# The gate unit's columns of the second half as seven block products in two passes

## The chip, the cores and the metric

One core of one Trainium2 chip runs the whole program. The metric is device time in microseconds (us): the median of the runs. Engines are TensorE (PE), VectorE (DVE), ScalarE (ACT), GpSimd (POOL) and SyncE (SP), which here issues nearly all DMAs.

## The reference, cut to what matters

One layer over 2048 latent tokens of width 1024 with a 256-token context ahead of it. One input projection `p = h @ w_in` with 3584 columns feeds two head groups:

```python
h = modulate(rmsnorm(x, norm_mix[l]), sh1, sc1)
p = h @ w_in[l]                       # 5 x 512 columns for the recurrence, 2 x 512 for the gate unit
...
def chunk_sgu(u, v, ln_g, ln_b, w_s, b_s):
    u = gelu(u); v = gelu(v)          # 4 heads of 128 channels, chunks of 128 positions
    v = layernorm(v, ln_g, ln_b)
    z = einsum('hpq,bnqhc->bnphc', w_s, v) + b
    return u * z
...
x = x + g1 * (o @ w_out[l])           # o: both groups side by side
x = x + g2 * conv_ffn(h2, ...)        # gated MLP with a 3x3 convolution
```

The other group (A) is a gated linear recurrence in both directions (four heads, 128 x 128 state). Only the gate unit's columns (B: u in columns 2560 to 3071, v in 3072 to 3583) change here, and of them only the second half of the tokens.

## The kernel before, in words

Everything is float32; a product that needs it is made of three `float32r` matmuls (`mm3`, L134): each operand is split (`split`, L129) into a high part (an ACT copy, L131) and a low part (a subtraction, L132), and high x high, high x low, low x high are summed in PSUM. A matmul takes 128 contraction rows, 128 columns of weights and 512 tokens.

The tokens are worked in two halves of 1024. For a half, `xh` and `xl` hold the normalised input's parts with the 1024 features on 8 blocks of 128 rows (NK = 8). **`x_second`** (L426) prepares half two while half one is being projected: in four groups of two token chunks it loads rows, scales them, transposes them on PE (64 transposes of 128 x 128), applies `a1`/`s1` (`x_mod`, L239), splits, and stores both parts in DRAM (`xh_d`, `xl_d`, L452). They are read back into `xh`/`xl` between the halves (L1074, L1075).

**The projection** runs as a list of banks (`run_banks`, L514). A bank is 512 tokens by 128 columns: 8 blocks x 3 matmuls = 24 matmuls into one of three `pj` PSUM banks, which a sink then evicts. Weights come raw from DRAM (`load_raw`, L211) and are split two keys ahead (`split_w`, L216). The banks' order is a string written by hand, for half two `f0 b0 f1 v0 b1 f2 u0 b2 f3 b3 v1 u1 v2 u2 v3 u3`: `f` is a recurrence head's front (gate `silu`, v, q: six banks, L977 to 978), `b` its back (forget gates: four banks), `v` and `u` the gate unit's two banks each.

**Two queues of generators** (`Pump`, L140s) are advanced at slots between the blocks of a bank, when PE's own counted time `T.t` has passed the wait that the generator yielded. `hg_q` holds the recurrence (`hg`, L776: scores by seven levels, states, output; `deferred`, L883: what half one's backward scan still lacks); each is posted at the start of the next front. `need` forces a queue ahead of its waits: `pre_q` needs the previous head's scores begun ("diag"), `pre_g` (ahead of the back) needs its keys, `pre_v` the end of the head before that. `bg_q` holds preparations: `x_start`, `misc`, `x_second`, then `ada_block` x8, `w_out_ops`, `conv_taps`, `w_down_ops`. A scheduler fixes each engine's order at build time by readiness in its model; `pin` keeps an instruction in program order.

**The gate unit** (`sgu`, L668): `su` evicts u by GELU, `sv` evicts v by GELU and queues `ln` after 4.6 us of `T.t` (transposes, statistics L694, L695, the root on POOL L126, normalisation L699) and then `mix` after 7.0 more (the position mixing on PE, L707); `both` multiplies on POOL (L675) and stores to `oT_d` (L676). Ahead of the second last pair of banks `open_wo` drains both queues, closes the pool of the recurrence's tiles and starts ten loads of the output projection's weights `wo` into that memory (L1106). Then comes the output projection, tile by tile (128 tokens), which fetches its operands with L1269.

PSUM has eight banks: three `pj`, two `sc`, three `mi`. Single or double buffers that matter: `raw` (three), `acc` (one), `sig` (two), `sgt` (two), `K` (two), `F` (one).

## Time and profile before

| | us |
|---|---|
| median of three runs (2453.74 to 2454.19) | 2453.82 |
| the profiled execution | 2449.13 |
| its span, first to last instruction | 2447.3 |
| half two's input stores (`xl_d`), first and last issue | 114.3, 201.9 |
| last matmul of the input projection | 977.3 |
| first load of the ten `wo` | 967.8 |

In a row of the grouped views stand line, engine, operation, tiles written and read, shapes and count, then busy time and mean ns of one, then the engine's idle time just before and who ended it. A row of windows has the length, then for PE, weight loads, DVE, ACT and POOL the busy time and count, then the granted clock, the DMA engines' busy share and GB/s. Matmuls are pipelined: their listed durations overlap, so their cost is read from how many fit in a stretch.

### The profile page before, as it was taken

What the parts mean: (1) busy time and instruction counts of PE and PEld (TensorE: products, weight loads), DVE (VectorE), ACT (ScalarE), POOL (GpSimd) and SP (SyncE); (2) the same over time, 40 slices, a digit from 0 to 9 for tenths busy, and PEclk for the clock granted to TensorE, in tenths of its full rate; (3) what the DMA queues carried; (4) which work ended last, traced back from release to release, by engine and by line L of the source; (5) the groups of instructions that cost most, each with busy time, mean ns of one, the idle gap of its engine ahead of it and who ended that gap; (6) DMA issues with size and microseconds to landing.
All of it is one profiled execution on the core that took longest, in us unless ns stands there. A gap on an engine that the chain in (4) does not pass through costs nothing.

```text
span 2447.3 us, 32836 instructions
## 1 busy us (share of the span) xinstructions
PE 2408.3 (98%) x11859; PEld 2000.8 (82%) x11859; DVE 1785.5 (73%) x2445; ACT 943.7 (39%) x1614; POOL 873.4 (36%) x795
## 2 busy tenths in 40 slices
PE   7999999999999999999999999999999999999998
PEld 4788888888888888788788888878888888888887
DVE  5867685756776776466698877769999992776875
ACT  4554334333344433354443333333333342332343
POOL 1232010110111122001688778787778870000002
PEclk9999999999999999999999999999999999999999
DMA  8365446564254234668822222562222238934645
GB/s 310 109 210 171 141 136 209 193 225 147 96 185 155 87 104 149 233 216 261 297 86 88 82 96 83 177 237 85 86 93 94 83 102 349 318 125 146 228 151 197
DMA packets 307855, 400.13 MB, mean 163 GB/s; under 512 B 33113, under 2 KB 216161, under 8 KB 304621
## 3 DMA queue, kind: packets, MB, share of 16 engines
q1 hardware_dynamic: 304404, 397.28, 48.1%
q8 instruction: 94, 1.54, 0.3%
q10 hardware_dynamic: 3289, 0.76, 0.1%
q14 instruction: 68, 0.56, 0.1%
HBM read 288.85 MB, written 109.13 MB: 163 GB/s over the span
## 4 chain that ended last, share of the span: by engine, by line
PE 40%; DVE 7%; issue 3%; POOL 2%; ACT 1%; DMA 0%; SPq 0%; POOLq 0%; ACTq 0%; DVEq 0%
PE up L65 25%; PE dn L65 15%; DVE dn L1377 3%; DVE edges L1382 1%; DVE gp L1458 1%; ACT dn L1374 1%; POOL Al L132 0%; POOL ra L1669 0%; POOL rr L1670 0%; DVE keep L1452 0%; POOL raw L1195 0%; DVE keep L1468 0%; ACT cv L1396 0%; ACT Ah L131 0%; POOL cv L1469 0%
## 5 line engine op out<-in xcount | busy, mean ns | idle before, releaser
L1377 DVE SCALAR_TENSOR_TENSOR dn<-gp,taps,dn 128x1024 f32<-128x1024 f32 x352 | 448.3, 1280 | 21.4 <-ACT dn L1374 18.1
L65 PE MATMUL up<-yf,Ah 128*128 128x512 f32 x1232 | 393.7, 389 | 0.0
L65 PE MATMUL dn<-thl,mhl 128*128 128x512 f32 x1680 | 381.5, 389 | 1.2 <-ACT thl L131 1.2
L132 POOL TENSOR_TENSOR Al<-raw,Ah 128x512 fp32r<-128x512 f32 x264 | 342.9, 1307 | 92.0 <-ACT Ah L131 79.0
L65 PEld LDWEIGHTS dn<-thl,mhl 128*128 128x128 f32 x1680 | 315.0, 188 | 67.7 <-ACT thl L131 2.0
L65 PE MATMUL pj<-xh,whi 128*128 128x512 f32 x896 | 363.1, 406 | 0.0
L65 PE MATMUL pj<-xh,wlo 128*128 128x512 f32 x896 | 350.6, 392 | 2.0 <-DVE wlo L132 2.0
L65 PE MATMUL pj<-xl,whi 128*128 128x512 f32 x896 | 351.4, 392 | 1.1 <-POOL xl L132 1.0
L65 PE MATMUL up<-xah,Al 128*128 128x512 f32 x704 | 275.6, 392 | 3.8 <-POOL Al L132 3.8
L65 PE MATMUL up<-xah,Ah 128*128 128x512 f32 x704 | 274.5, 390 | 0.6 <-ACT Ah L131 0.6
L65 PEld LDWEIGHTS up<-yf,Ah 128*128 128x128 f32 x1232 | 231.2, 188 | 48.1
L131 ACT CAST Ah<-raw 128x512 fp32r<-128x512 f32 x264 | 160.5, 618 | 278.4 <-PE up L65 208.4
L65 PE MATMUL up<-xal,Ah 128*128 128x512 f32 x528 | 205.5, 389 | 0.0
L65 PE MATMUL up<-yf,Al 128*128 128x512 f32 x528 | 205.2, 389 | 0.0
L65 PEld LDWEIGHTS pj<-xh,wlo 128*128 128x128 f32 x896 | 168.3, 188 | 38.2 <-DVE wlo L132 2.7
L65 PEld LDWEIGHTS pj<-xh,whi 128*128 128x128 f32 x896 | 168.6, 188 | 33.3 <-issue 3.5
L65 PEld LDWEIGHTS pj<-xl,whi 128*128 128x128 f32 x896 | 168.8, 188 | 32.2 <-POOL xl L132 1.9
L65 PE MATMUL dn<-wo,o 128*128 128x512 f32 x768 | 182.9, 394 | 2.1 <-ACT o L131 1.6
L580 POOL TENSOR_TENSOR K<-K,tot 128x512 f32<-128x512 f32 x40 | 50.0, 1251 | 343.9 <-PE sc L65 194.5
L65 PEld LDWEIGHTS dn<-wo,o 128*128 128x128 f32 x768 | 141.9, 188 | 31.8 <-ACT o L131 2.0
L65 PEld LDWEIGHTS up<-xah,Al 128*128 128x128 f32 x704 | 132.1, 188 | 36.5 <-POOL Al L132 9.4
L65 PEld LDWEIGHTS up<-xah,Ah 128*128 128x128 f32 x704 | 132.2, 188 | 28.0 <-ACT Ah L131 1.0
(315 smaller groups left out, 3923.7 us busy)
## 6 DMA issues: line engine op xcount, KB each, us to landing
raw<-in_w_up_dram SPq DMA_DIRECT2D x88, 512.0 KB, 4.7
mr<-m SPq DMA_DIRECT2D x85, 512.0 KB, 5.0
raw<-in_w_in_dram SPq DMA_DIRECT2D x68, 512.0 KB, 4.2
sT<-wd SPq DMA_DIRECT2D x88, 256.0 KB, 4.1
raw<-in_w_ada_dram SPq DMA_DIRECT2D x32, 512.0 KB, 3.8
yf<-yd SPq DMA_DIRECT2D x14, 1024.0 KB
m<-cv SPq DMA_DIRECT2D x22, 544.0 KB, 2.7
raw<-in_w_down_dram SPq DMA_DIRECT2D x22, 512.0 KB, 4.3
```

The lines of the kernel that those rows point to most:

```text
L65: return self.engine.matmul(out, lhsT, rhs, **kw)
L131: keep(S.copy(hi, raw))
L132: (eng or G).tensor_sub(lo, raw, hi.bitcast(F32))
L580: e.tensor_mul(view(K2, row * W + o, src), view(K, o, src), view(tot, t0, [[4, n], [ts, 2], [0, B]]))
L1374: S.activation(cr, gt[:, 0:RH, 0:GW], AF.Identity, bias=cvb[:, f:f + 1], scale=taps[:, f:f + 1])
L1377: V.scalar_tensor_tensor(out=cr, in0=gt[:, t // 3:t // 3 + RH, t % 3:t % 3 + GW], scalar=taps[:, t * NF + f:t * NF + f + 1], in1=cr, op0=A ...
L1382: V.scalar_tensor_tensor(out=e[:, 0, :], in0=gt[:, 1, t % 3:t % 3 + GW], scalar=taps[:, t * NF + f:t * NF + f + 1], in1=e[:, 0, :], op0=AL ...
L1458: V.tensor_add(g_rows(hh, f + c, n2), quad(p, kind), quad(add, kind))
```

## The change

For each gate head the two column groups (u, v) x the two halves of the 1024 features make a 2 x 2 block matrix of weights, and features x the two 512-token parts a 2 x 2 block matrix of inputs. Strassen's algorithm in Winograd's form takes seven block products of 12 matmuls in place of eight.

- `x_second` now takes chunks g and g + 4 together, forms the four sums and differences of input blocks next to the four blocks, splits all eight on DVE and stores them as eight operands (`xo_d`), 512-byte runs.
- `pair_ops`, new in `bg_q` ahead of the ada blocks, forms the seven weight operands per head, splits them and stores them (`sp_d`). `w_down_ops` yields 7.0 in place of 9.0.
- The recurrence's gate of half one goes straight to DRAM (`silu_out`); `x_second` and `pair_ops` use the `sgt` buffers in half one.
- Half two runs all recurrence heads first (the last with its gate columns at the end), then 28 products: pass one has products 0, 1, 2 of all heads, pass two 3, 4, 6, 5. Products load split weights three ahead and x quarters when the last user of the old ones is done. Partial sums (`u2_d`) and the finished u of the first part (`su_d`) wait in DRAM between the passes. `open_wo` comes ahead of the last seven products.

```diff
...
-    xh_d = dr.tile([P, NK, TH], F32, name="xh_d")
-    xl_d = dr.tile([P, NK, TH], F32, name="xl_d")
+    xo_d = dr.tile([P, 8, 2, 4, 512], F32, name="xo_d")
+    sp_d = [dr.tile([P, 7, 2, 512], F32, name=f"sp{h}") for h in range(NH)]
+    u2_d = [dr.tile([P, 512], F32, name=f"u2{h}") for h in range(NH)]
+    su_d = [dr.tile([P, 512], F32, name=f"su{h}") for h in range(NH)]
...
@@ -426,30 +428,41 @@
         def x_second():
 
             xk = pk.tile([P, 2, D], F32, tag="K", name="xk2", bufs=2, align_bytes=AL)
-            sp = pk.tile([P, 4, 512], F32R, tag="K", name="sp", bufs=2, align_bytes=AL)
+            sp = pk.tile([P, 2, 8, P], F32R, tag="K", name="sp", bufs=2, align_bytes=AL)
             xs = [xk[:, 0, :], xk[:, 1, :]]
             n = 0
-            for g in range(0, NCH, 2):
+            for g in range(NCH // 2):
...
-                    ld(xs[i], x_rows[NCH + g + i])
+                    ld(xs[i], x_rows[NCH + g + 4 * i])
...
-                for k in range(0, NK, 2):
+                cl = slice(g * P, g * P + P)
+                for k in range(4):
                     pt = bank("mi")
                     for kk in range(2):
                         for i in range(2):
...
-                            pin(T.transpose(pt[:, o:o + P], xk[:, i, (k + kk) * P:(k + kk + 1) * P], ident))
-                    b = 2 * (n % 2)
+                            kq = k + 4 * kk
+                            pin(T.transpose(pt[:, o:o + P], xk[:, i, kq * P:(kq + 1) * P], ident))
+                    lo = ph.tile([P, 8, P], F32R, tag="sgt", name="xf", bufs=2)
+                    fl = lo.bitcast(F32)
+                    for kk in range(2):
+                        kq = k + 4 * kk
+                        V.tensor_scalar(out=view(fl, 2 * kk * P, [[1, 256]]), in0=pt[:, kk * 256:kk * 256 + 256],
+                                        scalar1=a1[:, 0, kq:kq + 1], scalar2=s1[:, 0, kq:kq + 1],
+                                        op0=ALU.mult, op1=ALU.add)
+                    V.tensor_sub(view(fl, 4 * P, [[2 * P, 2], [1, P]]), view(fl, P, [[2 * P, 2], [1, P]]),
+                                 view(fl, 0, [[P, 2], [1, P]]))
+                    V.tensor_sub(fl[:, 5, :], fl[:, 3, :], fl[:, 4, :])
+                    V.tensor_sub(fl[:, 7, :], fl[:, 2, :], fl[:, 5, :])
+                    hi = sp[:, n % 2]
                     n += 1
-                    for kk in range(2):
-                        sl = slice(kk * 256, kk * 256 + 256)
-                        x_mod(pt[:, sl], 0, k + kk, sp[:, b, sl], sp[:, b + 1, sl], 256, V if kk else G)
-                    for t, d in ((0, xh_d), (1, xl_d)):
-                        st(d[:, k:k + 2, g * P:g * P + 256], sp[:, b + t, :].bitcast(F32).rearrange("p (k c) -> p k c", k=2))
+                    split(hi, lo, fl, V)
+                    st(xo_d[:, :, 0, k, cl], hi.bitcast(F32))
+                    st(xo_d[:, :, 1, k, cl], fl)
                     yield 2.2
 
...
-        def sgu(hh, h):
+        def sgu(hh, h, paired=False):
 
...
             def su(n0, n, pj):
-                u[n0] = pm.tile([P, 512], F32, tag="gu", name="gu", bufs=2)
-                S.activation(u[n0], pj, AF.Gelu)
+                t = pm.tile([P, 512], F32, tag="gu", name="gu", bufs=2)
+                S.activation(t, pj, AF.Gelu)
+                if paired and n0 == 0:
+                    st(su_d[h], t)
+                    return
+                u[n0] = t
                 both(n0)
 
             def sv(n0, n, pj):
...
+                    if paired and n0 == 0:
+                        u[n0] = pm.tile([P, 512], F32, tag="gu", name="gu", bufs=2)
+                        ld(u[n0], su_d[h])
...
-                st(sg_d[h], sgt)
...
-                    yield 9.0
+                    yield 7.0
...
+        def pair_ops():
+
+            for h in range(NH):
+                r0, r1 = (ph.tile([P, D], F32, tag="sgt", name="wr", bufs=2) for i in range(2))
+                for r, base in ((r0, 5), (r1, 6)):
+                    c0 = base * HW + h * P
+                    ld(r.rearrange("p (k c) -> p k c", c=P), w_in[:, c0:c0 + P].rearrange("(k p) c -> p k c", p=P))
+                yield 6.0
+                a11, a12, a21, a22 = r0[:, :512], r0[:, 512:], r1[:, :512], r1[:, 512:]
+                e = raw_tile()
+                e0, e1 = e[:, :512], e[:, 512:]
+
+                def put(i, t):
+                    hi = pm.tile([P, 512], F32, tag="acc", name="w_hi")
+                    split(hi.bitcast(F32R), t.bitcast(F32R), t, V)
+                    st(sp_d[h][:, i, 0], hi)
+                    st(sp_d[h][:, i, 1], t)
+                V.tensor_add(e0, a21, a22)
+                put(6, a22)
+                yield 2.0
+                V.tensor_sub(e1, e0, a11)
+                put(4, e0)
+                yield 2.0
+                V.tensor_sub(a21, a11, a21)
+                put(0, a11)
+                yield 2.0
+                put(3, a21)
+                yield 2.0
+                V.tensor_sub(a22, a12, e1)
+                put(1, e1)
+                yield 2.0
+                put(2, a12)
+                yield 2.0
+                put(5, a22)
+                yield 2.0
 
...
+        def silu_out(dst):
+            def f(n0, n, pj):
+                t = pm.tile([P, 512], F32, tag="sig", name="sig", bufs=2)
+                S.activation(t, pj, AF.Sigmoid)
+                V.scalar_tensor_tensor(out=t, in0=pj, scalar=1.0, in1=t, op0=ALU.mult, op1=ALU.mult)
+                st(dst[:, n0:n0 + n], t)
+            return f
+
...
-                t["sgt"] = ph.tile([P, TH], F32, tag="sgt", name="sgt", bufs=2)
+                t["sgt"] = ph.tile([P, TH], F32, tag="sgt", name="sgt", bufs=2) if hh else None
...
+                    bg_q.add(pair_ops())
...
-            front = tile_banks(4 * HW + h * P, lambda: silu(t["sgt"], 1.0), TH, pre_v)
-            front += tile_banks(2 * HW + h * P, lambda: sink_v(t["vt"]))
+            late = (hh, h) == (1, NH - 1)
+            front = tile_banks(4 * HW + h * P, lambda: silu(t["sgt"], 1.0) if hh else silu_out(sg_d[h]), TH,
+                               None if late else pre_v)
+            front += tile_banks(2 * HW + h * P, lambda: sink_v(t["vt"]), TH, pre_v if late else None)
             front += tile_banks(3 * HW + h * P, lambda: silu(t["qs"], float(P) ** -0.5), TH, pre_q)
...
-                ld(xh[:, k:k + 2, q:q + 512].bitcast(F32), xh_d[:, k:k + 2, q:q + 512])
-                ld(xl[:, k:k + 2, q:q + 512].bitcast(F32), xl_d[:, k:k + 2, q:q + 512])
+                for w, xt in enumerate((xh, xl)):
+                    ld(xt[:, k:k + 2, q:q + 512].bitcast(F32), xo_d[:, 2 * (k // 4) + q // 512, w, k % 4:k % 4 + 2])
 
         seq = []
-        for item in "f0 b0 f1 v0 b1 f2 u0 b2 f3 b3 v1 u1 v2 u2 v3 u3".split():
-            h = int(item[1])
-            if item[0] == "f":
-                front, back, head_post = head(1, h)
-                part = front
+        for h in range(NH):
+            front, back, head_post = head(1, h)
+            if h < NH - 1:
+                seq += with_post(front, post) + back
             else:
-                part = back if item[0] == "b" else sgu_part(1, h, item[0])
-            seq += with_post(part, post)
-            post = head_post if item[0] == "b" else lambda: None
+                seq += with_post(front[2:], post) + back + with_post(front[:2], head_post)
+            post = head_post
...
-        i = len(seq) - 4
-        pre0 = seq[i][4]
-
-        def wo_hook():
-            if pre0 is not None:
-                pre0()
-            nxt[seq[-1][0], 512] = split_w((seq[-1][0], 512))
-            open_wo()
-        seq[i] = (*seq[i][:4], wo_hook)
+
+        first = [(p, m) for p, m in ((0, 0), (1, 0), (0, 1), (0, 2), (1, 1), (1, 2))]
+        prods = [(c + p, m) for c in range(0, NH, 2) for p, m in first]
+        prods += [(0, 3), (1, 3), (0, 4), (0, 6), (0, 5), (1, 4), (1, 6), (1, 5)]
+        prods += [(p, m) for p in range(2, NH) for m in (3, 4, 6, 5)]
+        at, wops, xop = [], {}, {}
+        quarter = {0: (0, 0), 1: (0, 512), 2: (4, 0), 3: (0, 0), 4: (0, 512), 5: (4, 512), 6: (4, 0)}
+
+        def load_pair(n):
+            if n < len(prods):
+                p, m = prods[n]
+                t = p1.tile([P, 2, 4, P], F32R, tag=at[n % 4], name="wp", align_bytes=AL)
+                ld(t.bitcast(F32).rearrange("p w k c -> p w (k c)"), sp_d[p][:, m])
+                wops[n] = t
+
+        def load_x(m, op):
+            k, c = quarter[m]
+            for w, xt in enumerate((xh, xl)):
+                ld(xt[:, k:k + 4, c:c + 512].bitcast(F32), xo_d[:, op, w])
+
+        last = seq[-1]
+
+        def pairs_ahead():
+            at.extend(f"{t}{w_free[0]}" for t in ("whi", "wlo"))
+            load_pair(0)
+            load_pair(1)
+        seq[-1] = (*last[:4], pairs_ahead)
         run_banks(seq)
+        at.extend(f"{t}{w_free[1]}" for t in ("whi", "wlo"))
+        load_x(1, 5)
+        mix = {p: sgu(1, p, True) for p in range(NH)}
+        pbk, ut = {}, {}
+        ends = {m: max(n for n, e in enumerate(prods) if e[1] == m) for m in range(3)}
+        begun = min(n for n, e in enumerate(prods) if e[1] > 2)
+        opens = len(prods) - 7
+        for n, (p, m) in enumerate(prods):
+            if n == opens:
+                open_wo()
+            load_pair(n + 2 if n == 0 else n + 3)
+            if n == 0:
+                load_pair(3)
+            if m in (0, 1, 3, 4):
+                pbk[p, m] = bank("pj")
+            if m in (0, 3):
+                ut[p] = raw_tile().rearrange("p (a c) -> p a c", a=2)
+                if m == 3:
+                    ld(ut[p][:, 0, :], u2_d[p])
+            b = pbk[p, {0: 0, 1: 1, 2: 0, 3: 3, 4: 4, 5: 4, 6: 3}[m]]
+            w = wops.pop(n)
+            k0, c0 = quarter[m]
+            xs = [t[:, k0:k0 + 4, c0:c0 + 512] for t in (xh, xl)]
+            more = {"skip_group_check": True} if m in (2, 5, 6) else {}
+            for k in range(4):
+                if k:
+                    slot()
+                T.matmul(b, w[:, 0, k, :], xs[0][:, k, :], start=(k == 0 and not more), stop=False, **more)
+                T.matmul(b, w[:, 0, k, :], xs[1][:, k, :], start=False, stop=False, **more)
+                T.matmul(b, w[:, 1, k, :], xs[0][:, k, :], start=False, stop=(k == 3), **more)
+            u = ut[p]
+            su, sv = mix[p]
+            if m == 0:
+                S.copy(u[:, 0, :], b)
+            elif m == 1:
+                V.tensor_add(u[:, 0, :], b, u[:, 0, :])
+                st(u2_d[p], u[:, 0, :])
+            elif m == 2:
+                su(0, 512, b)
+            elif m == 3:
+                V.tensor_add(u[:, 1, :], b, u[:, 0, :])
+            elif m == 4:
+                V.tensor_add(u[:, 1, :], b, u[:, 1, :])
+                sv(512, 512, u[:, 1, :])
+            else:
+                V.tensor_add(b, b, u[:, 0, :])
+                (su if m == 5 else sv)(512 if m == 5 else 0, 512, b)
+            for m_, op in ((0, 6), (1, 4), (2, 7)):
+                if ends[m_] == n:
+                    load_x({0: 3, 1: 4, 2: 6}[m_], op)
+            slot()
         bg_q.drain()
         hg_q.flush()
```

## The prediction

> **What bounds the kernel now.** I read the page from the top: busy shares, the granted clock by slices, then the chain.
>
> ```profile
> span 2447.3 us, 32836 instructions
> ...
> PE 2408.3 (98%) x11859; PEld 2000.8 (82%) x11859; DVE 1785.5 (73%) x2445; ACT 943.7 (39%) x1614; POOL 873.4 (36%) x795
> ...
> PEclk9999999999999999999999999999999999999999
> ...
> PE up L65 25%; PE dn L65 15%; DVE dn L1377 3%; DVE edges L1382 1%; DVE gp L1458 1%; ACT dn L1374 1%; POOL Al L132 0%; POOL ra L1669 0%; POOL rr L1670 0%; DVE keep L1452 0%; POOL raw L1195 0%; DVE keep L1468 0%; ACT cv L1396 0%; ACT Ah L131 0%; POOL cv L1469 0%
> ```
>
> PE is busy for 98% of the span, at full clock. The chain has no line for the input projection (the `pj` banks), so it breaks off before the stage that changes and can't be used for it. Three other views settle that stage: a stretch in which PE does nothing but projection, PE's waits between 100 and 980 us, and the last 80 us before the out-projection.
>
> ```profile
> 758.20:767.00 8.80, 8.80 (x39) 7.17 (x39) 0.00 (x0) 1.51 (x3) 1.00 0.40 131
> ```
> ```profile
> PE sc L65 <- DVE Q L503: 2.0, 2, 1.3
> ...
> PE mi L69 <- DVE xk L237: 0.3, 1, 0.3
> ```
> ```profile
> 900.00:980.00 80.00, 76.74 (x460) 66.16 (x459) 52.87 (x116) 24.02 (x63) 20.75 (x24) 1.00 0.35 123
> ```
>
> The first row counts 39 matmuls of 512 columns in 8.80 us: one costs 8.80 / 39 = 0.226 us of PE time, though it is listed with some 0.39 us, because matmuls overlap. A full bank of 24 takes 5.4 us, one of the new products (12) 2.7 us. In the waits (the first and last of nine rows) PE waits some 7 us in all of 880 us. So up to the out-projection the time is the sum of PE's work; matmuls that go are worth their pitch. The last row has 80.00 - 76.74 = 3.3 us of idle PE, where `open_wo` forces out the rest of head 3.
>
> **The change part by part.**
>
> *Removed.* Each head's two column groups over two halves were 4 banks of 24 matmuls, 96; seven products of 12 make 84. Four heads save 48 x 0.226 = **10.8 us** of PE. Transposes stay the same in number (64 in `x_second`). With them go eight weight splits of half two on ACT and DVE. The Trainium skill, "TensorE: Matmul & The Clock Gate", section "Back-to-back issue gap", gives 131 ns as the sustained pitch at 512 columns; by that the 48 would be worth 6.3 us, an estimate. The measured 0.226 us decides here.
>
> *The input stage* (`x_second`, 16 steps, inside the first 205 us).
>
> ```profile
> 110.00:205.00 95.00, 94.34 (x531) 80.66 (x530) 65.98 (x149) 48.62 (x88) 32.34 (x35) 1.00 0.62 197
> ```
> ```profile
> L242 DVE TENSOR_SCALAR xfl<-mi,a,s 128x256 f32<-128x256 f32 x32 | 16.1, 532 | 5.3 <-POOL sp L132 3.2 <-PE mi L69 2.0
> L132 DVE TENSOR_TENSOR wlo<-raw,whi 128x1024 fp32r<-128x1024 f32 x12 | 14.6, 1219 | 9.2 <-ACT whi L131 9.2
> L132 DVE TENSOR_TENSOR sp<-xfl,sp 128x256 fp32r<-128x256 f32 x16 | 9.5, 592 | 1.9 <-ACT sp L131 1.9
> ```
> ```profile
> L131 ACT CAST sp<-xfl 128x256 fp32r<-128x256 f32 x32 | 12.9, 406 | 17.2 <-DVE xfl L242 11.3 <-issue 5.2
> L131 ACT CAST whi<-raw 128x1024 fp32r<-128x1024 f32 x12 | 12.6, 1048 | 15.8 <-PE pj L65 15.8
> ```
> ```profile
> L132 POOL TENSOR_TENSOR sp<-xfl,sp 128x256 fp32r<-128x256 f32 x16 | 18.2, 1138 | 27.3 <-ACT sp L131 27.3
> ```
> ```profile
> L1247 DVE TENSOR_TENSOR fl<-fl 128x256 f32<-128x256 f32 x28 | 13.6, 486 | 25.3 <-ACT fl L1244 25.3
> ...
> L1249 DVE TENSOR_TENSOR fl<-fl 128x128 f32<-128x128 f32 x27 | 9.9, 366 | 0.9
> ...
> L1248 DVE TENSOR_TENSOR fl<-fl 128x128 f32<-128x128 f32 x27 | 8.8, 325 | 0.7
> ```
> ```profile
> xh_d<-sp SPq DMA_DIRECT2D x16, 256.0 KB, 2.5
> ...
> yd<-yst SPq DMA_DIRECT2D x16, 448.0 KB, 4.5
> ```
>
> A step on DVE today: two scalings and one low part, 2 x 0.532 + 0.592 = 1.66 us; the other low part is POOL's. After: two scalings, three differences (the same shapes stand in the second norm's rows: 0.486 + 0.366 + 0.325) and one low part of 1024 columns (1.219), 3.46 us. That is +1.8 a step, 29 us for 16, and POOL's 18.2 us go. ACT has 1.05 for 0.81. DVE has 95.00 - 65.98 = 29 us idle here: the work just fits, with nothing left. The stores double, 32 of 512 KB in 512-byte runs, as the second norm's are: 4.5 x 512/448 = 5.1 us to landing for 2.5. With two buffers a step can't be shorter than (2 x 0.532 + 1.18 + 1.05 + 1.22 + 5.1) / 2 = 4.8 us. Four steps are 19 us, inside the 20.8 us that a group's yields give (6 + 6 + 4 x 2.2), so only the last group runs over, by some 8 us. What queues behind a late DVE is `silu`'s eviction and the weight's low part, and SP's weight loads behind a store that waits; PE meanwhile has three `pj` banks, 3 x 5.4 = 16.3 us, of head 0's gate columns, whose K tile waits for `x_second`'s buffers. Bounds: 0 (all in idle time) to 23 us (below, second rival); I take **+2**, near the lower end, since today's waits on this path are of tenths.
>
> *`pair_ops`* stands in the background queue where the ada blocks begin.
>
> ```profile
> L922 DVE SCALAR_TENSOR_TENSOR acc<-raw,cs,acc 128x512 f32<-128x512 f32 x64 | 49.1, 767 | 0.9 <-DMA raw<-in_w_ada_dram 0.5
> ```
> ```profile
> L971 SPq DMA_DIRECT2D wd<-raw x22: 513/525/629, 547.6 to 822.5; - x22
> ```
>
> Per head 4 sums and 7 low parts of 512 columns, 11 x 0.69 = 7.6 us of DVE in 20 us of yields; an ada block has 8 x 0.767 = 6.1 in 17.4. So DVE's load stays, and the tail moves: +80 us, less 22 x 2 for the shorter yields of `w_down_ops`, is 36 us. The last `wd` store goes from 822 to some 860 us, ahead of `open_wo`, which lies in the last 80 us before 980: hidden by some 40 us of slack at least. Its 56 stores and 8 loads move 19 MB more, 46 us at the peak rate below, in a stage where the DMA share is half; if that made weights late, their lead of two banks (10.9 us) covers a landing twice as long. **0**, at most 2. `silu_out` stores from its own tile; no engine gains work.
>
> *Half two up to the products.* The gate unit's banks no longer stand between a head's front and its back, so the previous head's level steps are forced out earlier.
>
> ```profile
> 835.56 0.73 DVE L807 COPY_PREDICATED sc<-msk,sc 128x512 f32<-128x512 uint8 x1 [0.61 <-PE sc L65]
> ...
> 839.61 0.74 DVE L807 COPY_PREDICATED sc<-msk,sc 128x512 f32<-128x512 uint8 x1
> ```
> ```profile
> L65 PE MATMUL sc<-Q,K 128*128 128x128 f32 x896 | 109.8, 275 | 2.0 <-DVE Q L503 2.0
> ```
>
> Following the yields of `hg`, two levels and the transposes are forced before b1 and b2, as before b3 today, and four levels and the transposes before the new b3 (its front is four banks, not six). A forced level takes 4.05 us (first row to second), DVE's time; four and the transposes 18 us. PE has 1.7 us of its own per level (109.8 / 64), 8.6 with the transposes, and three banks, 16.3: 24.9 us of cover. **0**; 9 us if nothing fills in. Today's b3 shows the filling: no wait of PE near 835 us. In exchange the forcing at the end goes: from head 3's `hg` to `open_wo` there are today 8 banks, 43.5 us; after, 2 banks and 21 products, 68 us, both plus some 28 us of the chain's own PE work (its levels alone are 109.8 / 8 = 13.7), against yields of 63 us and the same 28. So today it is forced and then it isn't: **-3** of the 3.3, at worst 0.
>
> *The products.*
>
> ```profile
> 510.00:515.00 5.00, 5.00 (x24) 4.14 (x23) 1.92 (x3) 1.75 (x3) 0.00 (x0) 1.00 1.05 407
> ```
> ```profile
> wo<-wo_d SPq DMA_DIRECT2D x10, 512.0 KB, 10.6
> ```
> ```profile
> L906 DVE TENSOR_TENSOR on<-mi,op 128x512 f32<-128x512 f32 x2 | 1.4, 686 | 0.0
> ```
>
> Each product loads 512 KB of split weights, 3 products (8.2 us) ahead; four 2 MB quarters of x come on top, of which the densest stretch (products 11 to 15) asks 5.3 MB in 18 us, against 407 GB/s: 13 us, enough. Five sums per head read PSUM (0.69 us each on DVE, 18% of a product's time) before the bank is written again one or two products later. The tight place is the end: `open_wo` issues ten 512 KB loads of `wo`, and the operands of the last three products come behind them on SP. Bounds: -1.1 (waits on split weights go) to +10.6 (one operand lands only after the ten); I take **+2**, since SP's order is by readiness and the operands are ready about when `wo`'s memory is.
>
> *The end.*
>
> ```profile
> 991.05 0.73 PE L65 MATMUL dn<-wo,o 128*128 128x512 f32 x2 [1.55 <-ACT o L131]
> 992.32 3.94 PE L65 MATMUL dn<-wo,o 128*128 128x512 f32 x16 [0.53 <-DVE o L132]
> ```
> ```profile
> 978.35 2.82 SPq L676 DMA_DIRECT2D oT<-nt  x2
> 981.26 0.57 SPq L1269 DMA_DIRECT2D raw<-oT  x1
> ```
> ```profile
> L65 PE MATMUL pj<-xh,wlo x896: 387/389/500, 69.4 to 977.3; 128*128 128x512 f32 x180
> ```
> ```profile
> L699 DVE TENSOR_SCALAR nt<-mi,mv,rs 128x128 f32<-128x128 f32 x8 | 2.7, 403 | 2.9 <-POOL rs L126 2.9
> L694 DVE BATCH_NORM_STATS2 bs<-mi 128x6 f32<-128x128 f32 x8 | 2.0, 272 | 0.0
> ...
> L707 DVE SCALAR_TENSOR_TENSOR nt<-mi,vec,rh 128x512 f32<-128x512 f32 x2 | 1.5, 746 | 1.5 <-PE mi L65 1.5
> ```
> ```profile
> L675 POOL TENSOR_TENSOR nt<-nt,gu 128x512 f32<-128x512 f32 x2 | 3.6, 1800 | 3.4 <-ACT o L131 2.2 <-issue 1.2
> L126 POOL TENSOR_TENSOR rs<-rs,mhalf 128x4 f32<-128x4 f32 x2 | 2.0, 1008 | 0.2
> ```
>
> Head 3's v is now finished one product before the end, so norm, mixing and store follow the last product: about 4 x 0.27 + 0.7 + 1.2 + 4 x 0.40 + 0.9 + 0.75 + 1.8 = 8 us, where today the last of the two stores is issued within 4 us (981.2, after the projection's last matmul at 977.3). The out-projection's second operand is fetched behind that store (981.26), and PE pays 1.55 + 0.53 us for it already. Against that, `wo` comes earlier, out of that fetch's way. From -2.1 to +5; **+1**.
>
> Sum: -10.8 + 2 + 0 + 0 - 3 + 2 + 1 = **-8.8 us**. The profiled execution took 2449.13 us (span 2447.3), so 2440.3 for it; the median of the runs is 2453.82, 4.7 above, and the forecast is made against that: **2445.0**. About 0.2%, 4.9 us, is what a measurement tells from no change.
>
> One row adds to any new stall:
>
> ```profile
> 29.00:32.00 3.00, 3.00 (x8) 0.84 (x8) 0.94 (x3) 1.74 (x4) 0.00 (x0) 0.51 1.15 333
> ...
> 988.00:992.00 4.00, 2.23 (x9) 1.22 (x7) 0.96 (x1) 1.04 (x1) 0.00 (x0) 1.00 1.05 336
> ```
>
> After the wait at 28 us the granted clock was 0.51 for 3 us; after the idle 1.8 us at 990 it stayed 1.00. A stall of several us can thus cost some 1.7 us more; the upper bounds above may be exceeded by that. The same skill page, section "What's actually happening", has half clock after one idle window of about 3.4 us; the first row shows it after less.
>
> **The rivals.**
> 1. *Weights late in the last seven products.* The ten `wo` loads come first on SP, and one operand lands only when they have, 10.6 us after PE could use it. For: the row of 10.6. Against: in today's order a `wo` load overtook the fetch of the first operand, so SP isn't held to program order. +10.6 for +2: 2453.6. Chance 0.16.
> 2. *Slower: DVE and its buffers in the input stage.* DVE's need becomes 66 + 27 = 93 of 95 us. If it fills only as well as today (66 / 95 = 0.69), the stage takes 93 / 0.69 = 134 us, 39 longer; PE covers 16.3 and pays 23. It decides once the stage grows by more than 16.3 us, and outweighs the gain from about 27. -10.8 - 3 + 23 + 2 + 1 = +12: 2466. Against: most of DVE's idle time today waits for POOL's low parts, which go. Chance 0.17.
> 3. *The end grows*: the fetch of the second operand is late by the full 5 us: 2449.0 and, with the clock's 1.7, 2450.7. Chance 0.07.
> 4. *The change takes out less PE time than it says*, because a matmul's pitch is shorter than 0.226 us (as if the weight load of the next were all that counts, 7.17 us for 39 in the first stretch, or 0.184): 48 x 0.184 = 8.8, or 2447.0. Chance 0.02, since 39 matmuls in 8.80 us speak against it. By the 131 ns of the Trainium skill's page named above the time would be 2449.5, an estimate; the trace doesn't agree.
>
> **How the numbers follow.** The forecast has 0.58, with its own range from 2437 (all lower bounds together give 2436.5) to 2448.9. Faster by over 0.2% are the forecast and rival 4: 0.60. Rivals 1 and 3 lie within 0.2%: 0.23. Rival 2 is slower: 0.17. The range that leaves out no more than 2 in 10 goes from 2437 to 2460, into the lower part of rival 2.
>
> **What would show it.** Right: `pj` matmuls fewer by 48 with the same pitch; no PE wait over 1 us between 110 and 230 us; no wait between the last head's chain and the products; PE's idle time in the 130 us before the out-projection under 5 us. Wrong: PE waiting for `xfl`-like tiles, K or a weight's low part before 230 us (rival 2); PE waiting for a DMA of the operands after the `wo` loads (rival 1); a gap over 3 us at the second tile of the out-projection (rival 3).

## The result and the profile after

The changed kernel takes **2524.01 us** (median of four runs, 2520.09 to 2525.36) where the kernel before took 2454.01 on the same chip (2453.74 to 2459.09). The ratio is 1.0278, 95% interval 1.026 to 1.0295: slower by 2.8%, some 68 us, where 2445.0 was forecast. The profiled execution took 2520.09 us, its span 2518.3.

The page of the changed kernel: the span, the engines, the granted clock in 40 slices, the chain by line.

```profile
span 2518.3 us, 33045 instructions
...
PE 2420.5 (96%) x11811; PEld 2005.0 (80%) x11811; DVE 1846.3 (73%) x2549; ACT 953.0 (38%) x1618; POOL 859.2 (34%) x779
...
PEclk9999989999999999899999999999999999999999
...
PE up L65 22%; PE dn L65 18%; DVE dn L1510 3%; DVE edges L1515 1%; DMA yd<-fl 1%; DMA raw<-in_w_up_dram 1%; POOL Al L134 1%; DVE gp L1591 1%; ACT dn L1507 1%; PE up L69 0%; POOL ra L1802 0%; ACT fl L1377 0%; DVE fl L134 0%; POOL rr L1803 0%; DVE cv L1443 0%
```

PE has 48 instructions fewer (11811 for 11859), as the change says, yet is busy 12 us longer, and its clock has two dips (the 6th and the 17th of the 40 slices) where before it had none. The chain again has no line for the projection. So I go by stretches: of the kernel before, from 110 us to the first matmul of the out-projection; then of the changed kernel.

```profile
110.00:978.40 868.40, 860.91 (x4925) 741.96 (x4923) 591.90 (x977) 339.83 (x655) 142.23 (x149) 1.00 0.47 157
```
```profile
538.86:547.66 8.80, 8.80 (x40) 7.31 (x39) 1.39 (x2) 2.04 (x4) 0.00 (x0) 1.00 0.93 289
110.00:205.00 95.00, 89.41 (x490) 75.22 (x489) 76.57 (x172) 48.06 (x65) 15.72 (x18) 0.98 0.75 224
205.00:300.00 95.00, 86.91 (x470) 73.08 (x469) 70.71 (x112) 42.87 (x71) 8.78 (x7) 0.98 0.64 208
300.00:400.00 100.00, 80.07 (x405) 65.42 (x404) 65.01 (x93) 31.45 (x50) 9.63 (x11) 0.90 0.59 184
900.00:1045.20 145.20, 120.16 (x660) 102.11 (x658) 85.86 (x195) 32.69 (x78) 30.41 (x36) 0.91 0.80 291
110.00:1045.20 935.20, 870.86 (x4869) 744.05 (x4867) 651.97 (x1078) 349.54 (x659) 129.36 (x133) 0.97 0.61 203
```

The first row is pure projection: 40 matmuls in 8.80 us, the pitch of before. The last row against that of before is the account. The out-projection begins 66.8 us later (935.20 - 868.40). PE's idle time grew from 7.5 to 64.3 us (+56.8), its busy time by 10.0; since 48 x 0.226 = 10.8 us of matmuls went, some 21 us of busy time are new. Most of it goes with the lower clock (0.97 for 1.00): taken over stretches of 1 us, busy time x (1 - granted clock) sums to 17.7 us. The other 3 us stay open. The idle time lies in four places: 5.6 us in the input stage (110 to 205), 8.1 (205 to 300) and 19.9 (300 to 400) where `pair_ops` runs, up to 336, and the ada blocks begin, and 25.0 from 900 us on (145.20 - 120.16), the products and the end. What PE waited for:

```profile
PE pj L65 <- ACT whi L133: 17.4, 3, 10.6
PE mi L65 <- DVE nt L719: 16.8, 5, 9.8
PE sc L65 <- DVE kd L798: 7.4, 2, 4.3
PE pj L65 <- DVE raw L1245: 4.4, 2, 3.0
PE mi L69 <- DVE xk L239: 4.4, 2, 3.4
PE mi L69 <- DVE nt L719: 2.8, 1, 2.8
```

The largest single wait, 10.6 us for a weight's high part at 319 us, on the timeline:

```profile
312.39 0.38 SPq L999 DMA_DIRECT2D wr<-in_w_in_dram  x1
312.83 0.58 SPq L215 DMA_DIRECT2D raw<-in_w_in_dram  x1
316.38 0.69 DVE L1010 TENSOR_TENSOR raw<-wr 128x512 f32<-128x512 f32 x1 [7.85 <-DMA wr<-in_w_in_dram]
...
319.11 0.79 PE L65 MATMUL pj<-xh,whi 128*128 128x512 f32 x1 [10.63 <-ACT whi L133]
```

SP asked for the projection's weights (L215) only at 312.83, right behind a load of `pair_ops` (L999) that stood on SP until its buffer was free. The next wait of this kind, 6.18 us ending at 352.56, comes after the last step of `pair_ops`: SP asked for those weights at 347.74, behind loads of an ada block. SP's own waits from 215 to 360 us and the issues of `pair_ops`' stores and of the last `wd` stores:

```profile
SPq L1008 <- ACT w_hi L133: 44.8, 26, 4.8
...
SPq L999 <- DMA sp<-wr: 10.2, 5, 3.1
```
```profile
L1008 SPq DMA_DIRECT2D sp<-w_hi x28: 319/320/1264, 223.7 to 336.0; - x28
```
```profile
L990 SPq DMA_DIRECT2D wd<-raw x22: 518/519/585, 691.2 to 933.4; - x22
```

28 steps in 112 us are 4.0 us a step on average, the waits for each head's loads included; undisturbed steps follow each other by 2.7 us (issues at 330.50, 333.23 and 336.00). Yielded were 2.0 a step (80 us in all with the 6.0 per head). The last `wd` store came at 933, not the forecast's 860. At the end of the products:

```profile
L1170 SPq DMA_DIRECT2D wo<-wo_d x10: 436/520/1322, 1003.0 to 1012.0; - x10
```
```profile
1005.95 6.78 SPq L1170 DMA_DIRECT2D wo<-wo_d  x9
...
1013.44 0.64 SPq L689 DMA_DIRECT2D oT<-nt  x1
...
1014.90 1.57 SPq L1189 DMA_DIRECT2D wp<-sp  x2
...
1023.21 1.37 DVE L719 TENSOR_SCALAR nt<-mi,mv,rs 128x128 f32<-128x128 f32 x4 [8.52 <-DMA oT<-nt]
1023.67 1.22 PE L65 MATMUL mi<-wsT,nt 128*128 128x128 f32 x4 [9.78 <-DVE nt L719]
```
```profile
1042.30 2.08 PE L65 MATMUL mi<-wsT,nt 128*128 128x128 f32 x8 [4.96 <-DVE nt L719]
1045.22 17.06 PE L65 MATMUL dn<-wo,o 128*128 128x512 f32 x63 [0.84 <-DVE nt L727]
```

Behind the ten loads of `wo` stands a 256 KB store. Its data were ready at 1006.1 us, when POOL's product ended, but SP spent 6.78 us on issuing nine of the loads first. The next norm needs the buffer that this store reads (`nt` has two), DVE stands for 8.5 us, PE for 9.8. After the last product the norm and the mixing of head 3 cost another 4.96 and 0.84. From there the out-projection runs 63 matmuls without a gap. The waits for `raw` (4.4 us) are waits for a PSUM bank that VectorE's sum frees. The longest, 2.98 us at 956, is not one of a transfer: the sum (L1245, 958.38) stands on VectorE behind the recurrence's scan of states (L793, from 955.40).

### The profile page after: what moved, and what is told of

The parts are those of the page before. It is cut to its first block, busy times and chain, and to the rows that moved or that the text cites. A ratio compares the mean times of both kernels' runs of the same rounds, so it can differ in the third digit from the quotient of the medians.

```text
span 2518.3 us, 33045 instructions
## 1 busy us (share of the span) xinstructions
PE 2420.5 (96%) x11811; PEld 2005.0 (80%) x11811; DVE 1846.3 (73%) x2549; ACT 953.0 (38%) x1618; POOL 859.2 (34%) x779
## 4 chain that ended last, share of the span: by engine, by line
PE 41%; DVE 8%; issue 4%; DMA 2%; POOL 2%; ACT 2%; SPq 0%; POOLq 0%; ACTq 0%; DVEq 0%
PE up L65 22%; PE dn L65 18%; DVE dn L1510 3%; DVE edges L1515 1%; DMA yd<-fl 1%; DMA raw<-in_w_up_dram 1%; POOL Al L134 1%; DVE gp L1591 1%; ACT dn L1507 1%; PE up L69 0%; POOL ra L1802 0%; ACT fl L1377 0%; DVE fl L134 0%; POOL rr L1803 0%; DVE cv L1443 0%
## 5 line engine op out<-in xcount | busy, mean ns | idle before, releaser
L65 PE MATMUL pj<-xh,whi 128*128 128x512 f32 x768 | 312.9, 408 | 17.4 <-ACT whi L133 17.4
L65 PE MATMUL pj<-xh,wlo 128*128 128x512 f32 x768 | 303.0, 395 | 1.8 <-DVE wlo L134 1.7
L65 PE MATMUL pj<-xl,whi 128*128 128x512 f32 x768 | 303.5, 395 | 0.9 <-POOL xl L134 0.8
L65 PEld LDWEIGHTS pj<-xh,whi 128*128 128x128 f32 x768 | 146.1, 190 | 46.8 <-ACT whi L133 18.0
L65 PEld LDWEIGHTS pj<-xh,wlo 128*128 128x128 f32 x768 | 145.3, 189 | 34.7 <-DVE wlo L134 2.9
L65 PEld LDWEIGHTS pj<-xl,whi 128*128 128x128 f32 x768 | 146.2, 190 | 28.5 <-POOL xl L134 1.7
```

What stands on the lines that cost most here:

```text
L65: return self.engine.matmul(out, lhsT, rhs, **kw)
```

## The experiments

Three theories for the three places. **A**: `pair_ops` asks for steps faster than its one buffer allows, so in-order engines stand in front of its operands, and weights queue behind (rival: VectorE or the DMA has no room for the work). **B**: the end waits behind the burst of `wo` (rivals: bandwidth taken by the products' operands; the place in the queue; the norm's own latency). **C**: the input stage is too heavy for VectorE (rival: its doubled stores). Ratios are against the kernel before on the same chip; "us" is (ratio - 1) x 2454.

| run | ratio (95% interval) | us |
|---|---|---|
| the change | 1.0278 (1.026 to 1.0295) | +68.2 |
| e1 half one as changed, half two as before | 1.0207 (1.019 to 1.0224) | +50.8 |
| e2 the same without `pair_ops` | 1.0038 (1.0023 to 1.0053) | +9.3 |
| e3 `pair_ops`' loads and stores on POOL's queue | 1.0366 (1.0351 to 1.0381) | +89.8 |
| e4 `pair_ops` paced 4.0 | 1.0251 (1.0236 to 1.0267) | +61.6 |
| e5 `wo` loads spread | 1.0252 (1.0237 to 1.0267) | +61.8 |
| e6 `wo` opened 3 products from the end | 1.0211 (1.0196 to 1.0226) | +51.8 |
| e7 one operand a head formed | 1.009 (1.0073 to 1.0107) | +22.1 |
| e8 as e2, stores as small as before | 1.003 (1.0019 to 1.0042) | +7.4 |
| e9 as e4, later background faster | 1.0176 (1.016 to 1.0191) | +43.2 |
| e10 `wo` loads on POOL's queue | 1.031 (1.0295 to 1.0324) | +76.1 |
| e11 as e6, store from u's buffer | 1.0216 (1.02 to 1.0231) | +53.0 |
| e12 as e9, waiting 12 for the loads | 1.0178 (1.0164 to 1.0192) | +43.7 |
| e13 as e2, half the low parts on POOL | 1.0062 (1.0049 to 1.0074) | +15.2 |
| e14 as e7, half the operands' bytes | 1.0073 (1.0057 to 1.009) | +17.9 |
| e15 `wo` opened 12 from the end | 1.027 (1.0256 to 1.0285) | +66.3 |
| e16 e12, e6 and e13 together | 1.0174 (1.0158 to 1.0189) | +42.7 |
| e17 e12 and e6 | 1.014 (1.0124 to 1.0155) | +34.4 |
| e18 as e17, `wo` in two blocks | 1.0139 (1.0122 to 1.0156) | +34.1 |

**Where the time is: e1, e2, e7.** e1 takes the hand-written order and the hook of before back into the changed kernel; e2 also leaves out `pair_ops`; e7 is the whole change with one operand a head: it leaves out forming the other six, and all seven products load that one.

```diff
-        for h in range(NH):
-            front, back, head_post = head(1, h)
+        for item in "f0 b0 f1 v0 b1 f2 u0 b2 f3 b3 v1 u1 v2 u2 v3 u3".split():
...
```
```diff
-                    bg_q.add(pair_ops())
```
```diff
-                ld(t.bitcast(F32).rearrange("p w k c -> p w (k c)"), sp_d[p][:, m])
+                ld(t.bitcast(F32).rearrange("p w k c -> p w (k c)"), sp_d[p][:, 6])
```

> Half one as changed (new input stage of x's second half, pair_ops, silu_out's stores), half two as before: the gate unit's columns go through the plain product with all 96 matmuls a head, and what pair_ops stores is not read. The three theories put the 70 us between the two traces in three places. If half one holds about 45 us of it (the input stage 14, pair_ops in SP's order 29, clock some more), this kernel takes 2490 to 2505 us, and PE's waits on the high parts of weights at 305 to 360 us stand as in the changed kernel. If the cause is the burst of weights of the out-projection and the last products alone, it takes 2454 to 2462 us.

> The same without pair_ops: of the change only the new input stage of x's second half and silu_out's stores stand, and half two is as before. If the input stage by itself costs what the excess over the pitch at 110 to 230 us grew by (2.4 to 16.6 us), this kernel takes 2464 to 2472 us. If the excess there came from pair_ops or from nothing but order, 2454 to 2458 us. The difference from the kernel with pair_ops is pair_ops' price: 25 to 40 us by the theory that its stores hold SP's queue, 0 to 2 us by the prediction.

> The changed kernel with pair_ops forming one operand a head instead of seven; every product loads that one, so that the products' result is not the gate unit's. Half two has all its products, loads, sums and stores. It should show half two without pair_ops and without its delay of the background work. If the waits of the products' stage (37 us of excess over the kernel before) are its own: 2461 (input stage alone) - 11 + 37 = 2487, 2480 to 2492. If they come from the background work, which pair_ops makes 110 us late and which then shares the DMA with the products: 2452 to 2464.

e1: +50.8, inside its first range, with the changed kernel's wait still there. From its waits of PE, 100 to 560 us:

```profile
PE pj L65 <- ACT whi L133: 16.1, 3, 10.7
```

e2: +9.3, between its two ranges. So `pair_ops` costs 50.8 - 9.3 = **41.5 us** with no product in the kernel (expected were 25 to 40), the input stage, with `silu_out`, **9.3**. e7: +22.1, a little under its range: with `pair_ops`' work all but gone and the `wd` stores done by 842 us, half two costs 22.1 - 9.3 = 12.8 us more than before instead of 10.8 less, so its own waits are worth **23.6**. They are the changed kernel's, from 860 us on:

```profile
PE mi L65 <- DVE nt L719: 14.9, 3, 9.2
PE pj L65 <- DVE raw L1223: 4.8, 2, 3.4
```

-10.8 + 9.3 + 41.5 + 23.6 = 63.6 of 68.2. Each run carries some 4 us of uncertainty, a difference of two some 6; the -10.8 is counted by the pitch, not measured by a run.

**What in `pair_ops`: e3, e4, e9, e12.** The queue, the pace, the speed of what follows, the wait for its loads.

```diff
-                    st(sp_d[h][:, i, 0], hi)
-                    st(sp_d[h][:, i, 1], t)
+                    G.dma_start(sp_d[h][:, i, 0], hi)
+                    G.dma_start(sp_d[h][:, i, 1], t)
```
```diff
                 put(6, a22)
-                yield 2.0
+                yield 4.0
```

> The changed kernel with pair_ops' loads and stores issued from POOL's queue instead of SP's; VectorE's work, the buffers and the bytes are the same. If what cost was that SP waits for pair_ops' high parts ahead of the weights' loads, PE's waits on the high parts of weights at 305 to 360 us (17.4 us in the changed kernel) go, and the time falls by 20 to 35 us to 2489 to 2504 us. If VectorE's load or the DMA bytes cost, it stays within 5 us of 2524 us; if POOL's queue is now what is held up (its own elementwise work stands behind the waiting stores), it is slower than 2524.

> The changed kernel with pair_ops' seven steps a head paced at 4.0 instead of 2.0, which is about the 3.7 us that one step took in the trace, so that a store is issued when its operand is nearly there and SP doesn't stand before it. By the theory of SP's queue the waits at 305 to 360 us shrink and the time falls by 15 to 30 us (2494 to 2509), with ada's blocks, which follow pair_ops in the background, no later than before. By the theory of VectorE's load: no change, within 5 us.

e3 is slower than the change by 21.6 us, so the theory of SP's queue as I had put it falls: PE still waits for high parts of weights. Rows of PE's waits from 215 to 400 us, and of ACT's from 215 to 370:

```profile
PE pj L65 <- ACT whi L133: 23.7, 3, 15.3
```
```profile
ACT w_hi L133 <- DMA sp<-w_hi: 38.7, 18, 6.3
ACT w_hi L133 <- DMA wr<-in_w_in_dram: 20.4, 3, 8.0
```

ACT itself stands before `pair_ops`' copies, whose one buffer waits for the last store or whose weights have not landed, and the projection's splits stand behind them on ACT, whatever queue the stores are on. The longest wait of PE, 15.3 us, ends at 345: SP had asked for the projection's weights at 330.84, but ACT splits them only at 343.98, behind two copies of `pair_ops`; before the first of them it stood for 9.5 us. POOL's queue is held up too, by 63.9 us of waits for ACT's copies, as the expectation's last branch has it; how the 21.6 us divide between the two isn't shown. In e4 the same steps take as long (118 us), SP waits as long, and PE no longer does; rows of e4's issues, of SP's waits from 215 to 400, of PE from 215 to 400 (the only one), and of its stretch at 300:

```profile
L1008 SPq DMA_DIRECT2D sp<-w_hi x28: 319/320/1159, 224.4 to 342.5; - x28
```
```profile
SPq L1008 <- ACT w_hi L133: 41.8, 25, 5.0
```
```profile
PE sc L65 <- DVE kd L798: 3.8, 1, 3.8
```
```profile
300.00:400.00 100.00, 100.00 (x566) 86.04 (x565) 68.14 (x101) 42.64 (x68) 11.49 (x11) 1.00 0.53 180
```

PE is full at 300 to 400 us where the change has 80.07, with about the same VectorE work (68.14 us for 65.01) and bytes (180 GB/s for 184): neither is the cause. What counts is what stands behind a step that can't start: at pace 2.0 SP issued the projection's weights at 280, 313 and 348 us, at 4.0 at 283, 295 and 320, between two steps. Yet the time fell by 6.6 us only, less than its range (the medians' 10.5 are of different chips), since all later background work moved back: the last `wd` store came at 994 us, amid the products, where PE waited 20.3 us for their operands.

```profile
L990 SPq DMA_DIRECT2D wd<-raw x22: 518/519/973, 736.0 to 994.1; - x22
```
```profile
PE pj L65 <- DMA wp<-sp: 20.3, 5, 13.8
```

e9 shortens the yields of that later work (first cut, against e4); e12 also changes `pair_ops`' own (second cut, against e9).

```diff
-            yield 7.0
+            yield 3.0
...
-                    yield 5.0
+                    yield 3.5
...
-                    yield 7.0
+                    yield 4.0
```
```diff
-                yield 6.0
+                yield 12.0
...
-                yield 4.0
+                yield 3.0
```

> pair_ops paced at 4.0 as in the run before of that name, and the background steps behind it shortened (3.0 for 7.0 after an ada block, 3.5 for 5.0 in the out-projection's weights, 4.0 for 7.0 in the down projection's), so that the same work is asked for some 115 us earlier by the yields. By the theory that late background work makes the products' stage wait, the excess before the out-projection (69.5 us at pace 4.0) falls by 25 to 45 us: 2470 to 2490. If VectorE or the DMA has no room for the same work in less time, waits show up at 340 to 900 us instead and it stays at 2505 to 2525.

> As the run with the faster rest (2499), but pair_ops waits 12 instead of 6 after asking for a head's two weight tiles, and 3.0 instead of 4.0 between steps: about the same length in all (132 and 136 by the yields). If VectorE and ACT standing in order before tiles not yet loaded is a part of the cost, the waits of PE at 225 to 235 us (5 us) go and the time falls by 3 to 8 us, to 2491 to 2496; if the pace of the steps against their one buffer is all, it is the same or, at 3.0 below the 3.7 that a step takes, slower by up to 10.

e9: 18.4 us below e4, less than the 25 to 45 expected, last `wd` store at 866 us; there was room for the work. What it leaves is some 9 us of PE's idle time when x is read back beside the background's transfers (515 to 600 us; 2.8 of them wait for x itself), the wait for `kd` at 228 us, and the end. e12: no difference. The wait for `kd` at 228 stays, 5.0 us in e12 and 3.9 in e9. In e12, 1.25 us of it are VectorE's first sum of `pair_ops` waiting for weights, whose loads SP held until the input stage's stores had left their buffers. In e9 that sum hardly waits; most of PE's wait is the gate's own chain, `F` on ACT, then `Q` and `kd` on VectorE with that sum between them.

**The input stage: e8, e13.** Stores as small as before, or half of each low part on POOL.

```diff
-                    st(xo_d[:, :, 0, k, cl], hi.bitcast(F32))
-                    st(xo_d[:, :, 1, k, cl], fl)
+                    st(xo_d[:, :4, 0, k, cl], hi.bitcast(F32)[:, :4])
+                    st(xo_d[:, :4, 1, k, cl], fl[:, :4])
```
```diff
-                    split(hi, lo, fl, V)
+                    S.copy(hi, fl)
+                    V.tensor_sub(lo[:, :4], fl[:, :4], hi[:, :4].bitcast(F32))
+                    G.tensor_sub(lo[:, 4:], fl[:, 4:], hi[:, 4:].bitcast(F32))
```

> The run with the input stage alone (half two as before), but of each step only the four plain quarters are stored, 256 KB instead of 512, as before the change; VectorE still forms the three sums and splits all eight. Half two there reads only the plain quarters. If the input stage's +9 us came from the doubled stores, which hold buffers and SP, it falls to +0 to +3 (2454 to 2457); if it came from VectorE's work, it stays at +7 to +10 (2461 to 2464).

> The run with the input stage alone (half two as before), but half of each step's low parts (512 of 1024 columns) is subtracted on POOL, as before the change; bytes, sums and stores are those of the change. VectorE's work in a step falls from 3.46 to some 2.9 us. If VectorE's work is the input stage's price, its +8 to +9 us fall to +3 to +6 (2456 to 2460); if the order of the steps or the tiles held is, it stays at +8 or, with POOL's slower half in the chain, grows to +15.

e8: +7.4 for +9.3, the same within their intervals: not the bytes. e13: +15.2, worse. The rows of e2 and e13 at 110 to 205 us:

```profile
110.00:205.00 95.00, 89.42 (x499) 75.29 (x498) 79.40 (x177) 48.25 (x65) 17.52 (x19) 1.00 0.81 245
```
```profile
110.00:205.00 95.00, 83.53 (x453) 70.20 (x452) 69.17 (x168) 43.83 (x60) 31.76 (x30) 0.95 0.76 225
```

VectorE is busy for 10 us less in e13 and PE idles 11.5 us instead of 5.6. So the stores don't set it, and a lighter VectorE alone doesn't help: e13 also made a step longer, with two tiles in flight (its last store came at 223.6 us, e2's at 214.3). As e13 changes both at once, VectorE's load isn't ruled out. Where PE stands in e2, of its 5.6 us:

```profile
PE mi L69 <- DVE xk L239: 4.3, 2, 3.4
```

`xk` are the scaled rows with which a group of four steps starts. The longest wait ends at 193.97: the rows' squares came on ACT only at 188.23, right behind the previous group's last copy, though SP had asked for the rows at 178.15. So the trace points at the passage from group to group, in the engines' order; no run tests it.

**The end: e5, e6, e15, e10, e11, e14.** When, in what portions, on which queue, from which buffer, against how many other bytes.

```diff
                         ld(wo[k][:, :, sl].bitcast(F32), wo_d[:, k, :, sl])
-                yield 17.0
+                        yield 2.0
+                yield 0.0
```
```diff
-        opens = len(prods) - 7
+        opens = len(prods) - 3
```

> The changed kernel, but the ten loads of the out-projection's weights go out 2 us apart instead of all at once. By the theory of the burst (small stores and the last operands land behind 5 MB of weights, PE waits 9.9 us at 1024 us and 5.1 at 1042) those waits shrink and the time falls by 8 to 15 us, to 2509 to 2516. If the bytes alone count, or the norm and mixing after the last product, it stays within 4 us of 2524.

> The changed kernel, but the out-projection's weights are opened for loading three products from the end instead of seven, so that all operands of products are asked for ahead of them. By the theory of the burst the wait for operands and stores goes, but the weights land some 11 us later and the out-projection may wait for them: 2512 to 2520 us. If the place makes no difference: 2524 within 4. If the weights of the out-projection are what PE waits for: slower than 2528.

> The changed kernel, but the out-projection's weights are opened twelve products from the end instead of seven (three gave 2508). If the 5 MB are best out of the way early, the last products' operands and stores go free and the time falls below 2520, to 2505 to 2518. If forcing head 3's chain out early costs PE, or the weights then stand in the way of more products, it is slower: 2525 to 2540.

e5: 6.4 us lower, under its range of 8 to 15, with intervals that just overlap. e6: 16.4 lower, clearly, and below its range; operands and loads of u are now asked for ahead of `wo`. PE's waits for `nt` from 860 us on fall from 15.5 to 9.4 us, but one of 9.0 stays. e15 (12 products from the end): no difference; its longest wait for `nt` is 9.7 us again, at 1012 us.

```diff
-                        ld(wo[k][:, :, sl].bitcast(F32), wo_d[:, k, :, sl])
+                        G.dma_start(wo[k][:, :, sl].bitcast(F32), wo_d[:, k, :, sl])
```
```diff
-                    G.tensor_mul(zt, zt, u.pop(n0))
-                    st(oT_d[hh][:, 4 + h, n0:n0 + 512], zt)
+                    gt = u.pop(n0)
+                    G.tensor_mul(gt, zt, gt)
+                    st(oT_d[hh][:, 4 + h, n0:n0 + 512], gt)
```

> The changed kernel, but the ten loads of the out-projection's weights are issued from POOL's queue instead of SP's: same bytes, same time, another queue. If the small store waits because it stands behind 5 MB in the same queue, it lands in 2 to 5 us, PE's wait of 9.9 us goes and the time falls by 7 to 14 us, to 2510 to 2517. If the DMA engines' bandwidth is what it waits for, whatever the queue, the time stays within 3 us of 2524.

> The run that opens the weights three products from the end (2508), and the product of normed v and u is written to u's buffer and stored from there, so that the buffer for the next norm is free once POOL has multiplied, not once the store has landed. If the 9.1 us wait left in that run is for a buffer held by a store behind the weights, it goes and the time falls by 6 to 10 us, to 2498 to 2502. If it is the norm's own latency, it stays at 2508 within 3.

e10 isn't faster, rather 8 us slower. SP now issues the norm's store at 1009.52, and the longest wait for `nt` falls from 9.8 to 4.1 us; but a wait of 14.4 us for a sum comes in its place, so leaving SP's queue doesn't help. A 256 KB load that SP issued at 1012.12, with `wo` on another queue, kept its reader until 1031.27:

```profile
1012.12 1.05 SPq L1223 DMA_DIRECT2D raw<-u  x1
...
1031.27 0.69 DVE L1245 TENSOR_TENSOR raw<-pj,raw 128x512 f32<-128x512 f32 x1 [15.81 <-DMA raw<-u]
```

The Trainium skill, "DMA: Bandwidth & Descriptors", section "Issuing engines are not separate DMA queues", says that transfers issued by different engines run on the same 16 DMA engines and interleave; that moving them gained nothing agrees with it. e11 has e6's time, but not for the reason expected in that case, the norm's latency. The wait moved from `nt` to u's buffer, on ACT, and the out-projection's first split (`o`) stood behind it:

```profile
1033.57 0.60 ACT L694 ACTIVATE gu<-pj 128x512 f32<-128x512 f32 x1 [13.00 <-DMA oT<-gu]
1034.07 1.04 ACT L133 CAST o<-raw 128x1024 fp32r<-128x1024 f32 x1
```

```diff
+                if n % 2:
+                    wops[n] = wops[n - 1]
+                    return
```

> The one-operand run (2477.6), but each loaded operand serves two products, so that 14 loads of 512 KB stand for 28 in the products' stage; all matmuls, sums and stores as there. If the DMA's bandwidth is what the stage waits for, the waits of PE at 919 and 981 us (3.5 and 9.3) shrink and the time falls by 5 to 12 us, to 2465 to 2472. If it is the moment at which the out-projection's weights are asked for, with their own 5 MB, or the norm after the last product, it stays at 2477 within 3.

e14: 4.2 us below e7 with overlapping intervals, between its two ranges. Its longest wait for `nt` stands at 9.9 us (9.2 in e7), so the operands' bytes don't make the large wait. The wait for `raw` is down from 3.4 to 0.7 us, but that doesn't speak for the bytes: in e7 the sum (L1223, 918.84) stands on VectorE behind the recurrence's scans of states, which run from 912.82 without a pause, and in e14 the sums come between these scans.

```profile
PE mi L65 <- DVE nt L719: 15.3, 4, 9.9
...
PE pj L65 <- DVE raw L1226: 0.7, 1, 0.7
```

**Together: e16, e17, e18.** e16 joins e12, e6 and e13, e17 leaves e13 out, e18 issues `wo`'s second column half 8 us later.

```diff
                 for n in range(2):
+                    if n:
+                        yield 8.0
```

> What helped, together: pair_ops waiting 12 for its weights and paced 3.0, the shorter background steps behind it, the weights opened three products from the end, half of the input stage's low parts on POOL. If the parts are separate the gains add: 2496.5 - 16 (opening late) - 3 to 5 (POOL) = 2475 to 2478, still above the kernel before, since the input stage, the reload of x beside the background's transfers and the end each keep some us and the 48 matmuls are worth 10.8. If they share one cause (DMA bytes), less: 2482 to 2492.

> pair_ops waiting 12 for its weights and paced 3.0, shorter background steps behind it, weights opened three products from the end; the input stage as in the change, with nothing on POOL. If half of the low parts on POOL cost the combined run what it cost alone (9 us), and opening late is worth what it was worth in the changed kernel (16), this takes 2480 to 2489 us. If opening late has no value once the background work is done earlier, 2494 to 2498.

> As the run before, but the ten loads of the out-projection's weights go out in two blocks of five, the columns that are used second 8 us after the first. If the norm's buffer and the last store wait behind the block as a whole, PE's wait of some 10 us before the out-projection falls to about half and the time by 3 to 8 us against that run. If the second block is then what the out-projection waits for, or the norm's own latency sets the end, it stays within 3 us of it or grows by up to 6.

e16 misses both its ranges; e17, inside its own, is 8.3 us faster and shows why: POOL's share in the input stage was a loss there too. e18 halves the wait at the end (PE for `nt`, from 860 us on, e17 and e18), so the block of `wo` is what holds it, but the time isn't clearly different (1.0139 for 1.014, where 3 to 8 us were expected).

```profile
PE mi L65 <- DVE nt L719: 8.9, 2, 8.5
```
```profile
PE mi L65 <- DVE nt L719: 4.4, 2, 2.7
```

The best version of the change is thus some 34 us behind the kernel before.

## Why the prediction was wrong

- *Matmuls removed, -10.8:* right. 48 fewer (11859 to 11811), 40 in 8.80 us.
- *`pair_ops`, "0, at most 2":* this step failed, by 41.5 us (e1 less e2). It compared VectorE's load and the lead of the weights with the landing of one transfer. The load was no problem (e4). A step's chain, copy, subtraction, store landing, with one `acc` buffer, takes 2.7 us undisturbed and 4.0 on average with the heads' loads, where 2.0 were yielded, and every in-order engine on the chain (SP, ACT, DVE) then stands before it with the projection's weights behind. The prediction had named neither that buffer nor what queues behind it. The tail followed: the last `wd` store at 933 instead of 860.
- *Half two up to the products, 0:* right: from 400 to 900 us PE idles 5.7 us where it idled 3.6 before.
- *The products, +2, and the end, +1, with -3 for the forcing that goes:* 23.6 us in all (e7 less e2 and the matmuls) instead of 0. Rival 1 had the mechanism, transfers that land only after the ten of `wo`, and its price, 10.6, is near the largest wait, 9.8. It had the wrong victim: not an operand but a store, whose buffer the norm needs. The norm and mixing behind the last product, costed at a few us beyond today's, are 4.96 + 0.84 of PE's wait: no matmul of the out-projection runs under them. Rival 3's place, the second operand, shows no gap. Nor did the waits around the recurrence's last steps go: 2.98 us at 956 behind its scans, and 2.8 at 990, where its transposes wait for a bank that a norm still reads.
- *The input stage, +2:* mis-sized, 9.3 (5.6 to 13.0), inside its bounds of 0 to 23. Its last store came at 214.6 us for 201.9. The reason given for the low value, that today's waits are tenths, says nothing of a stage whose step doubles.
- *The clock, 1.7 us a stall:* named as an addition and kept out of the sum; it made some 18 us (17.7).
- *Rival 2* had the sign, for a reason that gave little of the 68 us.

The common fault: each part was costed by the busy time that it adds against idle time that was there. The two large losses are mostly waits of an in-order engine for a buffer, a landing or the work ahead of it, with other work behind; in the input stage the trace points the same way, and no run shows it.

## What to carry to other kernels

Background work costs little by its busy time and much by its place: work out a step's chain through its buffers (copy, subtract, store landing, and the loads that it starts with), and pace the requests no faster, or the engines' order fills with instructions that can't start and the critical loads queue behind them. When a queue of background work is made longer, follow its tail into the stage where it now ends. Before a burst of large loads, list the small transfers that will be issued during it and which buffer each one holds. Before believing that a wait is one for a transfer, look at what the engine did until then.

## What the runs showed of the hardware

A long wait of PE costs more than its length. The two stretches right behind the 10.6 us wait of the changed kernel (the next three us are at 1.00 again):

```profile
319.00:322.00 3.00, 2.85 (x6) 1.84 (x7) 2.49 (x4) 0.67 (x2) 0.00 (x0) 0.50 0.94 293
322.00:325.00 3.00, 3.00 (x12) 2.35 (x11) 0.69 (x1) 0.62 (x1) 0.00 (x0) 0.74 0.91 267
```

The granted clock was 0.50 for 3 us and 0.74 for 3 more: 3 x 0.50 + 3 x 0.26 = 2.3 us on top. Summed over the stage, 56.8 us of added idle time brought some 18 us of slower work. The Trainium skill, "TensorE: Matmul & The Clock Gate", section "What's actually happening", has half clock after an idle window of about 3.4 us and full clock after as much sustained work; for this wait the trace agrees roughly: PE had stood since 308.48 when the clock fell to 0.50 (0.65 from 313 to 314 us), and it had worked since 319.11 when the clock came back (0.73 from 323 to 324). For shorter waits the trace differs: 2.65 us without work up to 602.62 were followed by 0.57 from 603 to 607, while 2.79 us up to 990.30 were followed by 1.00. So here the length of a wait alone didn't decide.

Issuing takes time as well: nine loads of 512 KB kept SP for 6.78 us. A queue of its own did not shield a transfer: with 5 MB of loads on POOL's queue, a 256 KB load on SP's took some 19 us to reach its reader (e10), with the DMA engines busy at a share of 0.99 from 1008 to 1030 us.
